# Moving most loads and the early stores of a 3x3 convolution to GpSimd's software DMA queue, each DMA as one packet per engine

## The chip, the core and the metric

The kernel runs on one core of a Trainium2 chip. The metric is the device time of one execution in microseconds. Three runs of the kernel before gave 122.27, 122.31 and 122.54 us; the median is 122.31 us.

The core has a matrix engine (TensorE, PE), a vector engine (VectorE, DVE), a scalar engine (ScalarE, ACT), a general engine (GpSimd, POOL) and an engine that here only issues transfers (SyncE, SP). Data moves between HBM and the on-chip memory (SBUF) through 16 DMA engines that all queues share. TensorE writes to a separate accumulator memory, PSUM.

## The reference

A 3x3 convolution with padding 1 over 16 images of 64 channels and 64x64 pixels, to 64 output channels, plus a residual. All inputs and the output are float32.

```python
def reference(x, weight, residual):
    x_pad = np.pad(x, ((0, 0), (0, 0), (1, 1), (1, 1)), mode='constant')
    for b in range(batch):          # 16
        for co in range(c_out):     # 64
            for ci in range(c_in):  # 64
                for kh in range(3):
                    for kw in range(3):
                        output[b, co] += weight[co, ci, kh, kw] * x_pad[b, ci, kh:kh+h, kw:kw+w]
    return output + residual
```

x, the residual and the output are 16.8 MB each, the weights 0.15 MB: 50.5 MB cross the DMA engines.

## The kernel before

**Tiles.** The 16 images are taken as 8 pairs. A tile of x is one pair: 128 rows (two images of 64 channels), one row of 4096 float32 (16 KB) in each partition, 2 MB in all. Three buffers `xr` hold x (`NXR = 3`), so x of pair p goes into the buffer that pair p - 3 had. The residual has room for all 8 pairs in one tile `ro`; the sum is made in place there, and the stores read it. The residual comes in seven DMAs, listed in `RES` (line 41): pair 0, pair 1, pairs 2 and 3, pairs 4 and 5, pair 6, and the two halves of pair 7. The output leaves in four early stores (`EARLY`, line 39: pairs 0-1, 2-3, 4-5, 6) and, at the end, the two halves of pair 7.

**Work of the engines.** POOL clears an identity matrix, the padding rows of the four bfloat16 tiles `xp`, and two parts of the weight tile `wl` (lines 163 to 179). TensorE turns the weights by nine transposes (line 233), and DVE (line 206) and ACT (line 199) copy the blocks to `wl`, together. For each of 16 images ACT casts x to bfloat16 in two halves, the even rows (line 190) and the odd rows (line 194); TensorE does 24 matmuls for it (lines 100 and 101 by way of a helper) into one of two PSUM tiles; DVE adds the residual in two halves (line 220).

ACT's queue is in this order: issue of residual 0, the two casts of image 0, the weight blocks, the casts of image 1, the casts of image 2, and so on. The casts of image 1 so come behind the weight blocks, and these behind the transposes, which wait for the weights (`s_w`). From image 4 on a cast also waits until TensorE is done with the image that had the same `xp` tile (`s_conv`).

**The order of the DMAs.** SP's queue carries nearly all of them, in the order of the code from line 144: x of pair 0 and, from ACT, residual 0, both put at the very front of the program by `to_the_front`; then the weights; then x of pair 1, residual 1, x of pair 2, x of pair 3, residual 2-3, x of pair 4, x of pair 5, residual 4-5, x of pair 6, x of pair 7, residual 6, residual 7 left, residual 7 right; then the early stores, which first wait for the next-to-last residual load (line 157). From pair 3 on the load of x waits for its buffer:

```python
nc.sync.wait_ge(s_half, 2 * (p - NXR) + 3)      # line 147
```

`s_half` counts ACT's first-half casts (line 190), one for each image. For pair 3 the wait is for 3: the first half of image 2 has been cast, so both images of pair 0 are done and `xr` 0 is free. For pair 4 it is 5, and so on. Each early store waits on `s_add`, which counts the adds of DVE (line 159). The two last stores stand behind the block of hand-ordered work (line 259), after all engines have come to its end; `s_out` counts the early stores, and POOL waits for it at the close (line 261).

Completion of a load is counted on a semaphore: `s_x` (one for each x buffer), `s_r` (three in turn), `s_w`.

Of the kernel before, what the change touches and what calls it, by code (L numbers as in the profile page):

```python
# [15 lines left out]
def kernel(  # L16
# [7 lines left out]
    nc = tc.nc  # L24
# [6 lines left out]
    NPIX = H * W  # L31
    NPAIR = B // 2
# [3 lines left out]
    NXR = 3  # L36
    NXP = 4
    NZERO = 4 + 2 * NXP
    EARLY = (slice(0, 2), slice(2, 4), slice(4, 6), slice(6, 7))
    WHOLE, LEFT, RIGHT = slice(0, NPIX), slice(0, NPIX // 2), slice(NPIX // 2, NPIX)  # L40
    RES = (
        (slice(0, 1), WHOLE, None),
        (slice(1, 2), WHOLE, 1),
        (slice(2, 4), WHOLE, 3),
        (slice(4, 6), WHOLE, 5),
        (slice(6, 7), WHOLE, 7),
        (slice(7, 8), LEFT, 7),
        (slice(7, 8), RIGHT, 7),
    )
    NR = 3  # L50

    res_bc = residual.rearrange("(p b) c h w -> (b c) p (h w)", b=2)
    out_bc = out.rearrange("(p b) c h w -> (b c) p (h w)", b=2)
    x_bc = x.rearrange("b c h w -> (b c) (h w)")
# [6 lines left out]
    ro = pool.tile([128, NPAIR, NPIX], FP32)  # L61
# [6 lines left out]

    sem = lambda name: tc.alloc_semaphore(name)
    s_w = sem("s_w")  # L70
    s_x = [sem(f"s_x{i}") for i in range(NXR)]
    s_r = [sem(f"s_r{i}") for i in range(NR)]
    s_out = sem("s_out")
    s_id = sem("s_id")
    s_half = sem("s_half")
# [2 lines left out]
    s_conv = sem("s_conv")  # L78
    s_add = sem("s_add")

    def load_x(p):
        return nc.sync.dma_start(out=xr[p % NXR][:, :], in_=x_bc[128 * p : 128 * p + 128, :]).then_inc(s_x[p % NXR], 16)

    def load_ro(i, e):
        pairs, cols, _ = RES[i]
        if i >= NR:
            e.wait_ge(s_r[i % NR], 16 * (i // NR))
        return e.dma_start(out=ro[:, pairs, cols], in_=res_bc[:, pairs, cols]).then_inc(s_r[i % NR], 16)

    def wait_ro(e, i):  # L90
        e.wait_ge(s_r[i % NR], 16 * (i // NR + 1))

    def store(pairs, cols=slice(0, NPIX)):
        return nc.sync.dma_start(out=out_bc[:, pairs, cols], in_=ro[:, pairs, cols])

    def matmul(out_, lhsT, rhs, start, stop, ldweights):

# [18 lines left out]
    def to_the_front(dma):  # L116

        def fixed(ap):  # L120
            t = ap.bass_ap.tensor.name
            return mybir.PhysicalAccessPattern(
                ap=ap.ap, offset=ap.bass_ap.offset, dtype=ap.dtype, memref=t, memsetref=t + "_set", bass_ap=ap.bass_ap
            )

        front = nc.main_func.blocks[0].instructions
        here = nc.cur_bb.bb.instructions
        ins = here.pop()
        assert ins.name == dma.ins.name
        at = next(i for i, e in enumerate(front) if e.engine == ins.engine)  # L130
        front.insert(at, copy.replace(ins, ins=[fixed(a) for a in ins.ins], outs=[fixed(a) for a in ins.outs]))
# [9 lines left out]

    with tc.tile_critical(no_gpsimd_drain=True):  # L142

        for p in range(NPAIR):
            if p >= NXR:

                nc.sync.wait_ge(s_half, 2 * (p - NXR) + 3)
            if p == 0:
                to_the_front(load_x(p))
                nc.sync.dma_start(out=wraw[:, :], in_=w_rows[:, :]).then_inc(s_w, 16)  # L150
            else:
                load_x(p)
            for i, (_, _, behind) in enumerate(RES):
                if behind == p:
                    load_ro(i, nc.sync)

        wait_ro(nc.sync, len(RES) - 2)
        for pairs in EARLY:
            nc.sync.wait_ge(s_add, 2 * pairs.stop + 1)
            store(pairs).then_inc(s_out, 16)  # L160


        nc.gpsimd.memset(ident[:, :], 0.0).then_inc(s_id, 1)  # L163
        nc.gpsimd.wait_ge(s_id, 1)
        nc.gpsimd.affine_select(  # L165
            out=ident[:, :],
            in_=ident[:, :],
            compare_op=mybir.AluOpType.not_equal,
            fill=1.0,
            base=0,  # L170
            pattern=[[-1, 128]],
            channel_multiplier=1,
        ).then_inc(s_id, 1)
        nc.gpsimd.wait_ge(s_id, 2)
        for t in xp:
            nc.gpsimd.memset(t[0:64, 0, :], 0.0).then_inc(s_id, 1)  # L176
            nc.gpsimd.memset(t[64:128, J, :], 0.0).then_inc(s_id, 1)  # L177
        nc.gpsimd.memset(wl[0:64, 0, :, 1, :], 0.0).then_inc(s_id, 1)  # L178
        nc.gpsimd.memset(wl[64:128, 1, :, 0, :], 0.0).then_inc(s_id, 1)  # L179


        to_the_front(load_ro(0, nc.scalar))
        for n in range(B):
            p, im = divmod(n, 2)
            hp = slice(64 * im, 64 * im + 64)
            x4 = xr[p % NXR].rearrange("q (j two w) -> q j two w", two=2, w=W)
            t = xp[n % NXP]
            if im == 0:
                nc.scalar.wait_ge(s_x[p % NXR], 16 * (p // NXR + 1))
            i = nc.scalar.copy(out=t[64:128, 0:J, :], in_=x4[hp, :, 0, :])  # L190
            i.then_inc(s_half, 1)
            if n >= NXP:
                i._wait_ge(s_conv, n - NXP + 1)
            nc.scalar.copy(out=t[0:64, 1 : J + 1, :], in_=x4[hp, :, 1, :]).then_inc(s_pack, 1)  # L194
            if n == 0:
                nc.scalar.wait_ge(s_id, NZERO + 1)
                for b in blocks[4:]:
                    for h in range(2):
                        i = nc.scalar.copy(**weight_block(h, *b))  # L199
                i.then_inc(s_id, 1)  # L200


        nc.vector.wait_ge(s_id, NZERO + 1)
        for k, b in enumerate(blocks[:4]):
            for h in range(2):
                i = nc.vector.tensor_copy(**weight_block(h, *b))  # L206
                if k == h == 0:
                    i.then_inc(s_bank, 2)
        i.then_inc(s_id, 1)
        for n in range(B):  # L210
            p, im = divmod(n, 2)
            hp = slice(64 * im, 64 * im + 64)
            o4 = ro[:, p, :].rearrange("q (j two w) -> q j two w", two=2, w=W)
            psj = ps[n % 2].rearrange("q c j w -> q (c j) w")
            if im == 0:
                for i, (pairs, cols, _) in enumerate(RES):
                    if pairs.start <= p < pairs.stop:
                        wait_ro(nc.vector, i)
            for par in range(2):
                i = nc.vector.tensor_tensor(  # L220
                    out=o4[hp, :, par, :], in0=psj[64 * par : 64 * par + 64, :, :], in1=o4[hp, :, par, :], op=ADD
                )
                if par == 0:
                    i._wait_ge(s_conv, n + 1)

                i.then_inc(s_add if par == 0 or n == B - 1 else s_bank, 1)


        nc.tensor.wait_ge(s_id, NZERO)
        nc.tensor.wait_ge(s_w, 16)  # L230
        wraw3 = wraw.rearrange("p (ci t) -> p ci t", t=9)
        for t in range(9):
            i = nc.tensor.transpose(  # L233
                out=tp[0:32, t // 3, 128 * (t % 3) : 128 * (t % 3) + 128], in_=wraw3[:, :, t], identity=ident[:, :]
            )
        i.then_inc(s_id, 1)
        nc.tensor.wait_ge(s_id, NZERO + 3)
        with nc.Fori(0, B // NXP, 1, engines=[PE]):
            for n in range(NXP):
                nc.tensor.wait_ge(s_bank, 1).then_inc(s_bank, -1)  # L240
                nc.tensor.wait_ge(s_pack, 1).then_inc(s_pack, -1)  # L241
                order = [(1, 0), (1, 1), (0, 0), (0, 1), (2, 0), (2, 1)]
                for i, (kw, d) in enumerate(order):
                    xlo, xhi = max(0, 1 - kw), min(W, W + 1 - kw)
                    for c in range(NCHUNK):
                        j0 = JC * c
                        m = matmul(
                            ps[n % 2][:, c, :, xlo:xhi],
                            wl[:, d, kw, :, :].rearrange("q r c -> q (r c)"),
                            xp[n][:, j0 + d : j0 + d + JC, xlo + kw - 1 : xhi + kw - 1],  # L250
                            i == 0,
                            i == len(order) - 1,
                            c == 0,
                        )
                m.then_inc(s_conv, 1)


    for cols in (LEFT, RIGHT):
        store(slice(NPAIR - 1, NPAIR), cols)
    with tc.tile_critical(sync_engine=mybir.EngineType.Pool, no_gpsimd_drain=True):  # L260
        nc.gpsimd.wait_ge(s_out, 16 * len(EARLY))
        tc.free_semaphores([s_w, *s_x, *s_r, s_out, s_id, s_half, s_pack, s_bank, s_conv, s_add])


# [28 lines left out]
```

## Time and profile before

| | before |
|---|---|
| median of three runs | 122.31 us |
| the profiled execution, its time | 122.44 us |
| the profiled execution, its span | 120.6 us |
| DMA | 50.48 MB in 3808 packets, mean 419 GB/s over the span |
| TensorE | 87.7 us busy, first transpose at 12.61 us, first matmul of the convolution at 18.12 us |
| last vector add ends | 108.6 us |
| mean granted TensorE clock | 0.952 |

The issues of the DMA view, with the time from issue to landing (median where there are several):

```profile
xr<-in_x_dram SPq DMA_DIRECT2D x8, 2048.0 KB, 14.4
out_dram<-ro SPq DMA_DIRECT2D x3, 4096.0 KB, 19.2
ro<-in_residual_dram SPq DMA_DIRECT2D x2, 4096.0 KB, 20.7
ro<-in_residual_dram ACTq DMA_DIRECT2D x1, 2048.0 KB, 12.0
wraw<-in_weight_dram SPq DMA_DIRECT2D x1, 144.0 KB, 11.4
```

"SPq" and "ACTq" are the queues of SP and ACT. A landing time counts from the issue until the DMA's semaphore is complete; it holds the time in which the DMA stands behind others. "q1" and "q10" on the page are the DMA queues that SP and ACT use. Engine names with a q at the end mean an engine's instruction queue. "GB/s" is what all DMA engines moved in one of 40 slices of the span; "DMA" is the tenths in which they were busy.

### The profile page before, as it was taken

Reading aid. Unit: us, or ns where it says so; the run is one execution under the profiler, and the core shown is the slowest. Engines: PE = TensorE matmul, PEld = TensorE weight load, DVE = VectorE, ACT = ScalarE, POOL = GpSimd, SP = SyncE. Lnnn points to the kernel's source line nnn. Section 1 sums busy time; section 2 is a strip of 40 time slices with the busy share of each in tenths; the row PEclk is TensorE's granted clock in tenths of the full one; section 3 lists DMA queues with packets and bytes.
Section 4 is the critical chain, followed back from the end, with each engine's and each line's share of the span. In section 5 each row is a group of like instructions: output and inputs, shape, how many; then the busy total and the mean of one; then the engine's idle time right before and its main releaser. Section 6 shows DMA issues by size and latency. Waiting matters only on the chain.

```text
span 120.6 us, 734 instructions
## 1 busy us (share of the span) xinstructions
PE 87.7 (73%) x389; PEld 10.7 (9%) x105; DVE 76.0 (63%) x40; ACT 63.1 (52%) x37; POOL 2.4 (2%) x16
## 2 busy tenths in 40 slices
PE   0000609999999999999999999999999999400000
PEld 0000300111101110101010101010101010000000
DVE  0000080039898898988989898898988989890000
ACT  4001999999988595875959578595800000000000
POOL 5200000000000000000000000000000000000000
PEclk9999999999999999999999999999999999995555
DMA  7999999999999999999999999999999999999994
GB/s 239 429 424 429 430 429 429 429 435 435 435 429 429 424 429 424 429 435 424 435 429 435 435 435 418 421 459 435 429 429 429 429 429 435 435 435 429 399 427 168
DMA packets 3808, 50.48 MB, mean 419 GB/s; under 512 B 352, under 2 KB 480, under 8 KB 480
## 3 DMA queue, kind: packets, MB, share of 16 engines
q1 hardware_dynamic: 3664, 48.38, 94.2%
q10 hardware_dynamic: 144, 2.10, 4.1%
HBM read 33.70 MB, written 16.78 MB: 419 GB/s over the span
## 4 chain that ended last, share of the span: by engine, by line
PE 71%; DVEq 2%; DVE 2%; issue 0%
PE ps L101 54%; PE ps L100 17%; DVEq L142 2%; DVE ro L220 2%
## 5 line engine op out<-in xcount | busy, mean ns | idle before, releaser
L220 DVE TENSOR_TENSOR ro<-ps,ro 64x2048 f32<-64x2048 f32 x32 | 73.2, 2288 | 17.7 <-PE ps L101 17.2
L101 PE MATMUL ps<-xp,wl 128*128 128x504 bf16 (+1 forms) x288 | 80.0, 388 | 0.2
L190 ACT CAST xp<-xr 64x2048 bf16<-64x2048 f32 x16 | 30.3, 1896 | 22.5 <-PE ps L101 13.1
L100 PE MATMUL ps<-xp,wl 128*128 128x504 bf16 (+1 forms) x92 | 35.9, 390 | 3.4 <-PEq L241 3.4
L194 ACT CAST xp<-xr 64x2048 bf16<-64x2048 f32 x16 | 30.4, 1898 | 0.4
L100 PEld LDWEIGHTS ps<-xp,wl 128*128 128x128 bf16 x96 | 9.5, 99 | 79.1 <-issue 79.1
L206 DVE CAST wl<-ps 32x192 bf16<-32x192 f32 x8 | 2.8, 348 | 14.9 <-PE ps L233 14.8
L233 PE MATMUL ps<-ident,wraw 128*32 128x128 f32 x9 | 2.1, 412 | 12.6 <-DMA wraw<-in_weight_dram 12.6
L233 PEld LDWEIGHTS ps<-ident,wraw 128*32 128x32 f32 x9 | 1.2, 137 | 13.0 <-issue 12.6
L190 ACT ACT_TABLE_LOAD x1 | 1.3, 1283 | 1.1 <-SPq L142 1.1
L199 ACT CAST wl<-ps 32x192 bf16<-32x192 f32 x4 | 1.2, 306 | 0.0
L177 POOL MEMSET xp<- 64x64 bf16 x4 | 0.6, 146 | 0.2
L176 POOL MEMSET xp<- 64x64 bf16 x4 | 0.6, 144 | 0.2
L165 POOL TENSOR_SCALAR_AFFINE_SELECT ident<-ident 128x128 f32<-128x128 f32 x1 | 0.3, 292 | 0.2 <-POOL ident L163 0.2
L179 POOL MEMSET wl<- 64x192 bf16 x1 | 0.3, 253 | 0.1
L178 POOL MEMSET wl<- 64x192 bf16 x1 | 0.3, 251 | 0.1
L163 POOL MEMSET ident<- 128x128 f32 x1 | 0.2, 204 | 0.7 <-SPq L142 0.7
L277 POOL MEMSET const-bfloat16-1.0<- 128x1 bf16 x1 | 0.1, 111 | 0.0
L277 POOL MEMSET const-uint8-127<- 128x1 uint8 x1 | 0.1, 111 | 0.0
L277 POOL MEMSET const-float32-1.0<- 128x1 f32 x1 | 0.1, 108 | 0.0
L277 POOL MEMSET const-float32-0.0<- 128x1 f32 x1 | 0.1, 103 | 0.2 <-issue 0.2
## 6 DMA issues: line engine op xcount, KB each, us to landing
xr<-in_x_dram SPq DMA_DIRECT2D x8, 2048.0 KB, 14.4
out_dram<-ro SPq DMA_DIRECT2D x3, 4096.0 KB, 19.2
ro<-in_residual_dram SPq DMA_DIRECT2D x2, 4096.0 KB, 20.7
ro<-in_residual_dram SPq DMA_DIRECT2D x2, 2048.0 KB, 18.1
ro<-in_residual_dram ACTq DMA_DIRECT2D x1, 2048.0 KB, 12.0
ro<-in_residual_dram SPq DMA_DIRECT2D x2, 1024.0 KB, 18.8
out_dram<-ro SPq DMA_DIRECT2D x1, 2048.0 KB, 13.7
out_dram<-ro SPq DMA_DIRECT2D x2, 1024.0 KB, 9.4
```

The source lines that it names most:

```text
L100: return e.matmul(out=out_, lhsT=lhsT, rhs=rhs, start=start, stop=stop, skip_group_check=True)
L101: return e.add_instruction(mybir.InstMatmult(name=nc.get_next_instruction_name(), engine=PE, ins=[e.lower_ap(rhs), e.lower_ap(lhsT)], outs ...
L142: with tc.tile_critical(no_gpsimd_drain=True):
L176: nc.gpsimd.memset(t[0:64, 0, :], 0.0).then_inc(s_id, 1)
L177: nc.gpsimd.memset(t[64:128, J, :], 0.0).then_inc(s_id, 1)
L190: i = nc.scalar.copy(out=t[64:128, 0:J, :], in_=x4[hp, :, 0, :])
L194: nc.scalar.copy(out=t[0:64, 1 : J + 1, :], in_=x4[hp, :, 1, :]).then_inc(s_pack, 1)
L199: i = nc.scalar.copy(**weight_block(h, *b))
L206: i = nc.vector.tensor_copy(**weight_block(h, *b))
L220: i = nc.vector.tensor_tensor(out=o4[hp, :, par, :], in0=psj[64 * par : 64 * par + 64, :, :], in1=o4[hp, :, par, :], op=ADD)
L233: i = nc.tensor.transpose(out=tp[0:32, t // 3, 128 * (t % 3) : 128 * (t % 3) + 128], in_=wraw3[:, :, t], identity=ident[:, :])
L277: nc = _bacc.Bacc("TRN2", target_bir_lowering=False, num_devices=1)
```

## The change

All DMAs behind the first two (x of pair 0 and residual 0) and the weights, up to and with the early stores, are issued by GpSimd and not by SP. GpSimd issues them behind its memsets, in the same order and with the same waits as SP did. A DMA that GpSimd issues [...]is marked `single_packet`: the share of each DMA engine in it is one packet. The two first loads get semaphores of their own (`s_x0`, `s_r0`), so that no semaphore counts DMAs of both kinds. SP keeps x of pair 0, the weights, and the two stores of pair 7.

```diff
+    s_x0, s_r0 = sem("s_x0"), sem("s_r0")
+    s_x = [sem(f"s_x{i}_sw") for i in range(NXR)]
+    s_r = [sem(f"s_r{i}_sw") for i in range(NR)]
...
+    def dma(e, out, in_):
+        return e.dma_start(out=out, in_=in_, single_packet=e is nc.gpsimd)
+
+    def at_x(p):
+
+        return (s_x[p % NXR], 16 * ((p - 1) // NXR)) if p else (s_x0, 0)
+
+    def at_ro(i):
+        return (s_r[i % NR], 16 * ((i - 1) // NR)) if i else (s_r0, 0)
+
+    def load_x(p, e):
+        return dma(e, xr[p % NXR][:, :], x_bc[128 * p : 128 * p + 128, :]).then_inc(at_x(p)[0], 16)
 
     def load_ro(i, e):
         pairs, cols, _ = RES[i]
+        s, before = at_ro(i)
+        if before:
+            e.wait_ge(s, before)
+        return dma(e, ro[:, pairs, cols], res_bc[:, pairs, cols]).then_inc(s, 16)
...
+    def store(pairs, cols, e):
+        return dma(e, out_bc[:, pairs, cols], ro[:, pairs, cols])
...
-        for p in range(NPAIR):
-            if p >= NXR:
-
-                nc.sync.wait_ge(s_half, 2 * (p - NXR) + 3)
-            if p == 0:
-                to_the_front(load_x(p))
-                nc.sync.dma_start(out=wraw[:, :], in_=w_rows[:, :]).then_inc(s_w, 16)
-            else:
-                load_x(p)
-            for i, (_, _, behind) in enumerate(RES):
-                if behind == p:
-                    load_ro(i, nc.sync)
-
-        wait_ro(nc.sync, len(RES) - 2)
-        for pairs in EARLY:
-            nc.sync.wait_ge(s_add, 2 * pairs.stop + 1)
-            store(pairs).then_inc(s_out, 16)
+        to_the_front(load_x(0, nc.sync))
+        nc.sync.dma_start(out=wraw[:, :], in_=w_rows[:, :]).then_inc(s_w, 16)
...
         nc.gpsimd.memset(wl[64:128, 1, :, 0, :], 0.0).then_inc(s_id, 1)
+        for p in range(1, NPAIR):
+            if p >= NXR:
+
+                nc.gpsimd.wait_ge(s_half, 2 * (p - NXR) + 3)
+            load_x(p, nc.gpsimd)
+            for i, (_, _, behind) in enumerate(RES):
+                if behind == p:
+                    load_ro(i, nc.gpsimd)
+
+        wait_ro(nc.gpsimd, len(RES) - 2)
+        for pairs in EARLY:
+            nc.gpsimd.wait_ge(s_add, 2 * pairs.stop + 1)
+            store(pairs, WHOLE, nc.gpsimd).then_inc(s_out, 16)
...
             if im == 0:
-                nc.scalar.wait_ge(s_x[p % NXR], 16 * (p // NXR + 1))
+                s, before = at_x(p)
+                nc.scalar.wait_ge(s, before + 16)
...
     for cols in (LEFT, RIGHT):
-        store(slice(NPAIR - 1, NPAIR), cols)
+        store(slice(NPAIR - 1, NPAIR), cols, nc.sync)
```

More of the change, by code (lines that the diff above doesn't have):

```diff
@@ L70 @@
     s_w = sem("s_w")
-    s_x = [sem(f"s_x{i}") for i in range(NXR)]
-    s_r = [sem(f"s_r{i}") for i in range(NR)]
+    s_x0, s_r0 = sem("s_x0"), sem("s_r0")
+    s_x = [sem(f"s_x{i}_sw") for i in range(NXR)]
+    s_r = [sem(f"s_r{i}_sw") for i in range(NR)]
     s_out = sem("s_out")
@@ L79 @@
     s_add = sem("s_add")
-    def load_x(p):
-        return nc.sync.dma_start(out=xr[p % NXR][:, :], in_=x_bc[128 * p : 128 * p + 128, :]).then_inc(s_x[p % NXR], 16)
+    def dma(e, out, in_):
[6 more added lines that the diff above has]
+        return dma(e, xr[p % NXR][:, :], x_bc[128 * p : 128 * p + 128, :]).then_inc(at_x(p)[0], 16)
     def load_ro(i, e):
         pairs, cols, _ = RES[i]
-        if i >= NR:
-            e.wait_ge(s_r[i % NR], 16 * (i // NR))
-        return e.dma_start(out=ro[:, pairs, cols], in_=res_bc[:, pairs, cols]).then_inc(s_r[i % NR], 16)
+        s, before = at_ro(i)
+        if before:
+            e.wait_ge(s, before)
+        return dma(e, ro[:, pairs, cols], res_bc[:, pairs, cols]).then_inc(s, 16)
     def wait_ro(e, i):
-        e.wait_ge(s_r[i % NR], 16 * (i // NR + 1))
-    def store(pairs, cols=slice(0, NPIX)):
-        return nc.sync.dma_start(out=out_bc[:, pairs, cols], in_=ro[:, pairs, cols])
+        s, before = at_ro(i)
+        e.wait_ge(s, before + 16)
+    def store(pairs, cols, e):
+        return dma(e, out_bc[:, pairs, cols], ro[:, pairs, cols])
     def matmul(out_, lhsT, rhs, start, stop, ldweights):
@@ L258 @@
     for cols in (LEFT, RIGHT):
-        store(slice(NPAIR - 1, NPAIR), cols)
+        store(slice(NPAIR - 1, NPAIR), cols, nc.sync)
     with tc.tile_critical(sync_engine=mybir.EngineType.Pool, no_gpsimd_drain=True):
         nc.gpsimd.wait_ge(s_out, 16 * len(EARLY))
-        tc.free_semaphores([s_w, *s_x, *s_r, s_out, s_id, s_half, s_pack, s_bank, s_conv, s_add])
+        tc.free_semaphores([s_w, s_x0, s_r0, *s_x, *s_r, s_out, s_id, s_half, s_pack, s_bank, s_conv, s_add])
 _INS = ['x', 'weight', 'residual']
```

## The prediction, made before the changed kernel ran

> **What bounds the kernel now.** I read the page's parts 1 to 3 first, then the DMA view by window, then the timeline of the first 24 us, because the chain of waits alone misleads here.
>
> The page, parts 1 to 4:
>
> ```profile
> span 120.6 us, 734 instructions
> PE 87.7 (73%) x389; PEld 10.7 (9%) x105; DVE 76.0 (63%) x40; ACT 63.1 (52%) x37; POOL 2.4 (2%) x16
> ...
> DMA  7999999999999999999999999999999999999994
> ...
> q1 hardware_dynamic: 3664, 48.38, 94.2%
> q10 hardware_dynamic: 144, 2.10, 4.1%
> ...
> PE 71%; DVEq 2%; DVE 2%; issue 0%
> ```
>
> No compute engine is busy over 73%, while the 16 DMA engines are in the top digit in all slices but the first and the last. The chain ends in TensorE work only because it stops at the last vector add (108.7 us); the 12 us behind that are stores. 50.48 MB at the 431 GB/s that the windows view gives for 20 to 100 us are 117.1 us; first byte and last receipt make up the 120.6. So the span is the time to move the bytes, and it grows by every microsecond in which the DMA engines have nothing queued. The question is whether the change makes such a gap.
>
> The DMA view of 3 to 10 us, while two queues compete:
>
> ```profile
> DMA packets 180, 2.95 MB, mean 421 GB/s; under 512 B 0, under 2 KB 0, under 8 KB 0
> ## 3 DMA queue, kind: packets, MB, share of 16 engines
> q1 hardware_dynamic: 96, 1.57, 52.4%
> q10 hardware_dynamic: 84, 1.38, 46.0%
> ```
>
> q1 is SP, with x of pair 0; q10 is ACT, with residual 0. They get packet for packet (1.57 MB / 96 = 16.4 KB, one row of a tile), although SP issued first: the engines take turns.
>
> The timeline of 11 to 24 us (start, duration):
>
> ```profile
> 11.54 1.90 ACT L190 CAST xp<-xr 64x2048 bf16<-64x2048 f32 x1 [9.19 <-DMA xr<-in_x_dram]
> ...
> 12.61 2.08 PE L233 MATMUL ps<-ident,wraw 128*32 128x128 f32 x9 [12.61 <-DMA wraw<-in_weight_dram]
> 13.46 1.90 ACT L194 CAST xp<-xr 64x2048 bf16<-64x2048 f32 x1
> 14.80 2.89 DVE L206 CAST wl<-ps 32x192 bf16<-32x192 f32 x8 [14.80 <-PE ps L233]
> 15.27 1.26 ACT L199 CAST wl<-ps 32x192 bf16<-32x192 f32 x4
> 16.55 1.89 ACT L190 CAST xp<-xr 64x2048 bf16<-64x2048 f32 x1
> 18.12 0.59 PE L100 MATMUL ps<-xp,wl 128*128 128x512 bf16 x1 [3.44 <-PEq L241]
> 18.46 1.90 ACT L194 CAST xp<-xr 64x2048 bf16<-64x2048 f32 x1
> 20.39 1.90 ACT L190 CAST xp<-xr 64x2048 bf16<-64x2048 f32 x1
> 22.31 0.33 SPq L82 DMA_DIRECT2D xr<-in_x_dram  x1
> ```
>
> This is the loop that keeps the DMA fed. Weights land at 12.5; transposes; block copies on DVE and ACT; ACT casts image 1 and the first half of image 2; that third count of s_half releases x of pair 3 (22.31). By the DMA view's issues x of pair 2 lands at 2.58 + 24.5 = 27.1: when pair 3 is issued, some 4.4 us of work is still queued (27.1 less 0.4 for the receipt: in the trace's packet records the weights' last packet is at 12.1, their landing at 12.5). That is the whole margin.
>
> **What the Trainium skill says.** "DMA: Bandwidth & Descriptors", section "Queues, rings and completion order": each DMA engine goes round the queues that have work and drains a whole packet of one before it switches. The trace agrees for packets of one row (96 against 84 above); no packet of many rows is in it. The same page, "Latency and other measured facts": first byte about 0.6 us on the hardware path, about 1 us on GpSimd's. In the trace the first hardware bytes come 1.0 us after issue; the software path is not in it. The same page, "Why small descriptors are slow": about 3 cycles per packet. "SBUF — State Buffer", "SBUF: two separate sides": VectorE in a 2-port mode, or with two SBUF inputs against a GpSimd read, can hold GpSimd off its descriptors. Line 220 reads one operand from PSUM and takes 2288 ns for 2048 elements, so I see no such mode, and cost that at nothing.
>
> **The change, part by part.** Sums are against the profiled execution: span 120.6 us, its time 122.44, so 1.84 us lie around the span; the median of the runs is 122.31, 0.13 lower.
>
> 1. Of SP's 21 DMAs 17 go to POOL (seven of x, six of the residual, four early stores), in the same order with the same waits. SP keeps x of pair 0, the weights and the two last stores; ACT keeps residual 0. Bytes are unchanged.
>
> 2. POOL first does its memsets, which end at 4.04 us. SP issued x1, r1 and x2 at 1.5 to 3.0 us. With about 1 us to first byte the new queue has work at 5 to 6 us. x0, r0 and the weights are 4.34 MB, 10 us of DMA work from 1.0 us on, so this later start alone leaves no gap. Cost nothing; if GpSimd took over 7 us more for its first DMA, the cover is gone.
>
> 3. What competes with the weights. Before, x1, r1 and x2 stood behind x0 and the weights on the same queue. Now they are on a third queue. One row takes 16384 B / (431/16 GB/s) = 0.61 us on an engine; a whole x tile is 8 rows per engine, 4.9 us, and now one packet. At 5.5 us about four of eight rows of x0 are through. From there each engine gives POOL 4.9 us, then one row to SP and one to ACT, then POOL again. SP needs at least a dozen more turns (the rest of x0, its semaphore write, eight 1152 B weight rows, theirs), and POOL has three packets before it stops at s_half. So POOL drains x1, r1 and x2 first, and the weights are last of the six transfers. The six take as long as before, so the last lands near 27.1: weights at 27.1 instead of 12.5 (1.11 + 11.4), plus 14.6. The last row of x0 comes behind the third packet: 6 + 3 × 4.9 + six rows of 0.61 = 24.4, 25 with the receipt, instead of 11.5.
>
> 4. The loop behind it, by the durations above: transposes 27.2 to 29.3; ACT has by then cast image 0 (25 + 3.8 = 28.8) and goes on at 29.4: block copies 1.26, then three casts of 1.90 and their gaps, 5.75: third count of s_half at 36.4 (22.3 before). GpSimd's first byte 1.0 later: 37.4. The queues had run dry at 27.1 − 0.4 = 26.7. Gap: 10.7 us, with nothing beside it.
>
> 5. What is late next. TensorE starts 14.3 us late (29.4 + 2.9 = 32.3), ends at 118.3, the adds at 123.0. The DMA is late by 10.7. Every later wait keeps its cover: x4 needs s_half near 44.1 (29.99 + 14.1) and the queue is full to 52.0 (37.4 + 4.9 + 9.7 for pairs 2 and 3 of the residual); early store 4:6, issued at 90.74, moves to 105.0, and the store ahead of it lands at 78.8 + 21.4 + 10.7 = 110.9. The last two stores are issued at about 123.0 and 123.6; one alone needs some 3.4 us, so 127; the bytes end later, at 119 + 10.7 = 129.7 (in the windows view nothing moves behind 119.0). The DMA stays the bound.
>
> 6. One packet instead of many rows. The nearest bounds: nothing, or 3 cycles at the page's 0.85 GHz, 3.5 ns, per row. POOL moves 44 of 50.48 MB, 168 rows per engine: 0.6 us. I take −0.5, an estimate. The other way, the page's "Measured" section has 425 GB/s for 16 MB on GpSimd's path; 44 MB take 103.5 us so, 102.1 at 431: 1.4 us slower. Neither is in the trace.
>
> 7. SP loses its waits; nothing else stood behind them. POOL's waits stand before nothing but its own DMAs and the closing wait on s_out.
>
> Sum: 120.6 + 10.7 − 0.5 = 130.8 span, + 1.84 = 132.6 us.
>
> **Rivals.**
>
> Row by row (20%): the one-packet mark doesn't make engines hold the turn, and three queues share by rows. Then x0's rest costs 9 turns (to 11.9), its semaphore write and r0's last row 4 (14.3), and each of eight weight rows waits for one POOL row, 5.3 us: 19.6, landing 20.0, 7.5 late. s_half reaches three near 29.2, first byte 30.2, gap 3.5: 122.44 + 3.5 = 125.9 us. For it: the trace shows turns of one row. Against: its DMAs have one row per packet, and the change asks for another packet.
>
> Not slower (10%): the turn is not even; an engine serves SP's and ACT's queues first and POOL's only when they are empty. It decides from the point where POOL gets no turn on an engine before the last weight row, at about 12 us. Then x0 and the weights land as before, POOL's three packets fill the time behind them as SP's did, the loop closes at 22.3, and only item 6 is left: 122.44 − 0.5 = 121.9 us. For it: the page on order speaks of even turns, but no view shows a software queue beside a hardware one. Against: the two hardware queues got even turns although one was first.
>
> Slower still (8%): the gap as forecast, and the software queue also moves less (item 6's 1.4 us instead of a gain) or writes descriptors too late to stay ahead: 134.5 to 138.
>
> **How the numbers follow.** 62% for the forecast: 132.6, its own range 130 to 134.5 (one us to first byte could be 0.5 to 2; item 6 both ways). Range: down to 124.5, to hold the row-by-row case, and up to 135: it leaves out the 10% that is not slower and part of the 8%. What a measurement here can tell from no change is 0.2%, 0.25 us. Faster 0.08, within 0.03, slower 0.89.
>
> **What would show it.** PE's first transpose near 27 us instead of 12.6; a hole of about 10 us in the DMA and GB/s rows from 27 to 37; POOL's x of pair 3 issued at about 36; full DMA digits behind that; packets per queue far fewer, or much larger. A transpose near 20 us means rows in turn; one at 12.6 means I am wrong about who competes. If the DMA row has no hole but GB/s stand under 425, the software path's rate is the cause.

## The result, and the profile after

The changed kernel takes 127.75 us (median of four runs, 127.58 to 127.77), beside 122.38 us for the kernel before (here of four runs): 1.0435 times as long, 95% interval 1.0417 to 1.0453. It is slower by 5.4 us. The profiled execution took 127.76 us, with a span of 125.4.

From the page of the changed kernel, parts 1 to 3 (the rows of slices have 3.1 us for each digit):

```profile
span 125.4 us, 734 instructions
PE 87.6 (70%) x389; PEld 10.7 (9%) x105; DVE 76.0 (61%) x40; ACT 63.2 (50%) x37; POOL 12.4 (10%) x33
...
DMA  7999999934999999999999999999999999999994
GB/s 230 428 423 428 431 437 423 428 162 115 392 423 434 444 428 439 423 423 428 439 439 434 428 418 434 418 405 410 481 428 423 418 423 418 470 434 423 395 442 178
...
q0 software_dynamic: 3088, 44.04, 82.7%
q1 hardware_dynamic: 576, 4.34, 8.6%
q10 hardware_dynamic: 144, 2.10, 3.9%
```

q0, which the page calls software_dynamic, is GpSimd's queue; q1 is SP's and q10 ACT's, as before. TensorE, VectorE and ScalarE are as busy as before, in microseconds; GpSimd has 10 us more, the issuing of its DMAs; the bytes are the same. The DMA row, which had a 9 in every slice but the ends, now has a 3 and a 4: a hole between 25 and 31 us. The windows view of the changed kernel puts a size on it (after the window come the busy times of PE, PEld, DVE, ACT and POOL; the last three columns are the granted clock, the DMA share and GB/s):

```profile
26.80:30.80 4.00, 4.00 (x12) 0.40 (x3) 0.00 (x0) 3.95 (x3) 1.23 (x2) 1.00 0.25 49
30.80:124.00 93.20, 79.58 (x366) 8.88 (x91) 73.24 (x32) 48.99 (x26) 7.15 (x12) 0.95 1.00 425
124.00:125.40 1.40, 0.00 (x0) 0.00 (x0) 0.00 (x0) 0.00 (x0) 0.00 (x0) 0.50 0.00 0
```

Four microseconds move 49 GB/s, about a ninth of what comes behind them; afterwards the DMA engines are full again until 124.0 (119.0 before), and the tail is as long as before. The hole's cause stands in the timeline of the first 30 us (start, duration):

```profile
4.02 0.68 POOL L83 DMA_DIRECT2D xr<-in_x_dram  x1
4.70 0.54 POOL L83 DMA_DIRECT2D ro<-in_residual_dram  x1
5.23 0.53 POOL L83 DMA_DIRECT2D xr<-in_x_dram  x1
13.41 1.90 ACT L202 CAST xp<-xr 64x2048 bf16<-64x2048 f32 x1 [11.05 <-DMA xr<-in_x_dram]
...
19.38 2.08 PE L245 MATMUL ps<-ident,wraw 128*32 128x128 f32 x9 [19.38 <-DMA wraw<-in_weight_dram]
21.50 1.27 ACT L211 CAST wl<-ps 32x192 bf16<-32x192 f32 x4 [4.27 <-PE ps L245]
...
22.79 1.90 ACT L202 CAST xp<-xr 64x2048 bf16<-64x2048 f32 x1
...
24.90 0.59 PE L113 MATMUL ps<-xp,wl 128*128 128x512 bf16 x1 [3.44 <-PEq L253]
...
26.63 1.90 ACT L202 CAST xp<-xr 64x2048 bf16<-64x2048 f32 x1
...
28.82 0.53 POOL L83 DMA_DIRECT2D xr<-in_x_dram  x1 [23.06 <-ACT xp L202]
```

The weights, which landed at 12.5 before, let TensorE go at 19.38. ACT sat idle for 4.27 us before its weight blocks, and the casts behind them came late by nearly as much as the weights: the transposes are 6.8 us late, and x of pair 3 was issued 6.5 us late, at 28.82 instead of 22.31. By then the first six transfers had been over for 2 us.

Why the weights are late is seen in the DMA view of 8.3 to 13 us of the changed kernel (queue: packets, MB, share):

```profile
DMA packets 141, 2.06 MB, mean 439 GB/s; under 512 B 15, under 2 KB 15, under 8 KB 15
...
q0 software_dynamic: 47, 0.77, 38.2%
q10 hardware_dynamic: 47, 0.77, 38.2%
q1 hardware_dynamic: 47, 0.52, 26.2%
```

Three queues get the same number of packets. A packet of GpSimd's queue is 0.77 MB / 47 = 16.4 KB, one row, although its DMAs are marked as one packet. SP's turns here still carry x of pair 0; its small ones are semaphore writes. In the packet records the weights' rows then stand one by one, each behind a 16 KB row of GpSimd's queue.

### The profile page after: what moved, and what is told of

Read it like the earlier page. It is cut to its first block, busy times and chain, and to the rows that moved or that the text cites. A ratio compares the mean times of both kernels' runs of the same rounds, so it can differ in the third digit from the quotient of the medians.

```text
span 125.4 us, 734 instructions
## 1 busy us (share of the span) xinstructions
PE 87.6 (70%) x389; PEld 10.7 (9%) x105; DVE 76.0 (61%) x40; ACT 63.2 (50%) x37; POOL 12.4 (10%) x33
## 2 busy tenths in 40 slices
DMA packets 3808, 50.48 MB, mean 402 GB/s; under 512 B 352, under 2 KB 480, under 8 KB 480
## 3 DMA queue, kind: packets, MB, share of 16 engines
q0 software_dynamic: 3088, 44.04, 82.7%
## 4 chain that ended last, share of the span: by engine, by line
PE 68%; DVEq 2%; DVE 2%; issue 0%
PE ps L114 52%; PE ps L113 16%; DVEq L155 2%; DVE ro L232 2%
## 5 line engine op out<-in xcount | busy, mean ns | idle before, releaser
L83 POOL DMA_DIRECT2D xr<-in_x_dram x7 | 3.9, 560 | 56.8 <-ACT xp L202 56.8
L83 POOL DMA_DIRECT2D out_dram<-ro x4 | 2.7, 679 | 37.6 <-DVE ro L232 22.5
L83 POOL DMA_DIRECT2D ro<-in_residual_dram x6 | 3.5, 590 | 0.0
```

The lines of the kernel that those rows point to most:

```text
L83: return e.dma_start(out=out, in_=in_, single_packet=e is nc.gpsimd)
```

## The experiments

### Does the mark matter?

```diff
-        return e.dma_start(out=out, in_=in_, single_packet=e is nc.gpsimd)
+        return e.dma_start(out=out, in_=in_, single_packet=False)
```

> The changed kernel with the one-packet mark taken off GpSimd's DMAs. If the mark does nothing to the turns of the DMA engines and nothing to the rate (the changed kernel's records show rows of 16 KB in turn on three queues): the weights land near 19.3 us, the hole in the DMA is the same, 127.7 us (within 0.3). If the mark does hold the turn for several rows, or saves time per row, without it the weights land earlier or the full stretches get slower: a change of 0.5 us or more either way.

Measured: 127.79 us (127.63 to 127.99), beside 127.75 for the changed kernel: no difference. The hole is the same: 157 and 94 GB/s in the two low slices of its page. The same question on the hardware path, first with the weights alone marked:

```diff
-        nc.sync.dma_start(out=wraw[:, :], in_=w_rows[:, :]).then_inc(s_w, 16)
+        nc.sync.dma_start(out=wraw[:, :], in_=w_rows[:, :], single_packet=True).then_inc(s_w, 16)
```

> The changed kernel with the one-packet mark also on the weights' DMA, which SP issues. If a marked DMA is one turn on the hardware path: its eight rows of an engine go in one turn and not in eight, the weights land about 4.2 us earlier (near 15.1), the third count of s_half near 24.4, no hole, 122.9 to 123.5. If the mark changes no turns on the hardware path either: weights at 19.3, 127.7.

Measured: 127.58 us (127.35 to 127.98); the timeline of this run has

```profile
19.20 2.08 PE L245 MATMUL ps<-ident,wraw 128*32 128x128 f32 x9 [19.20 <-DMA wraw<-in_weight_dram]
```

so the weights came when they came unmarked. And with all x, residual and output DMAs of the kernel before marked, on their hardware queues:

```diff
-        return nc.sync.dma_start(out=out_bc[:, pairs, cols], in_=ro[:, pairs, cols])
+        return nc.sync.dma_start(out=out_bc[:, pairs, cols], in_=ro[:, pairs, cols], single_packet=True)
...
```

> The kernel before with the one-packet mark on all loads of x and of the residual and on the stores, all still on the hardware queues of SP and ACT (the weights unmarked). If the mark saves the gap between rows (one row each 607 ns in the records[...]): up to 0.9 us less, 121.4. If a marked DMA is one turn, x of pair 0 (or residual 0) comes in one piece, so x lands at about 7 us or stays near 11.5. If the mark does nothing: 122.34, landings as before.

Measured: 122.33 us (13 runs) beside 122.43 for before (17 runs), ratio 0.9992, interval 0.9983 to 1.0000. Its DMA view of 3 to 10 us:

```profile
q1 hardware_dynamic: 96, 1.57, 52.4%
q10 hardware_dynamic: 89, 1.46, 48.7%
```

Rows still alternate, as in the kernel before. With rows of 16 KB (and of 1152 B for the weights) the mark changed neither turns nor rate on either path. Whether the request gets lost, or the engines don't heed it, no run here tells.

### Is it the software queue, or who stands beside the weights?

The three loads that competed with the weights go back to SP, behind the weights; GpSimd issues all from x of pair 3 on. They have semaphores of their own.

```diff
         nc.sync.dma_start(out=wraw[:, :], in_=w_rows[:, :]).then_inc(s_w, 16)
+        load_x(1, nc.sync)
+        load_ro(1, nc.sync)
+        load_x(2, nc.sync)
...
-        for p in range(1, NPAIR):
+        for p in range(NXR, NPAIR):
```

> The changed kernel with x of pairs 1 and 2 and residual 1 back on SP, behind the weights; GpSimd issues everything from x of pair 3 on, marked. Theory A (the loss is the hole in the DMA between 26.8 and 30.7 us, because the weights share turns with GpSimd's first three loads): weights land at 12.5, x of pair 3 is issued at 22.4, no hole or one under 1 us, and the time is that of before plus at most 0.6 us that lies outside the span: 122.4 to 123.0. Theory C (GpSimd's queue moves less, or pauses at each wait): 124 or more, with holes or lower GB/s behind 30 us.

Measured: 122.41 us (122.26 to 122.53, 13 runs), ratio to before 1.0004, interval 0.9996 to 1.0012. GpSimd's queue then carries the later loads and the early stores at the old pace: no digit of the DMA row is under 9 between the ends.

```profile
DMA  6999999999999999999999999999999999999994
GB/s 217 429 435 422 437 429 435 435 424 424 435 429 435 435 435 429 424 429 429 435 429 435 435 429 405 432 451 429 435 435 429 429 424 424 418 435 424 435 421 187
```

So the software queue costs nothing that shows in the steady part. The other way round, all of GpSimd's DMAs stay and the weights move to ACT's queue, ahead of residual 0, which so loses its place at the very front of the program:

```diff
-        nc.sync.dma_start(out=wraw[:, :], in_=w_rows[:, :]).then_inc(s_w, 16)
...
-        to_the_front(load_ro(0, nc.scalar))
+        nc.scalar.dma_start(out=wraw[:, :], in_=w_rows[:, :]).then_inc(s_w, 16)
+        load_ro(0, nc.scalar)
```

> The changed kernel with the weights issued by ACT ahead of residual 0 (both behind the start of the program, at 1.1 and 1.5 us); GpSimd's DMAs stay as they are and still compete with x of pair 0. Theory A: weights land near 3 us, x of pair 0 near 11, third count of s_half near 22, no hole, 122.4 to 123.0. Theory C (the software queue itself costs, wherever the weights stand): 125 or more.

Measured: 123.49 us (123.40 to 123.70). x of pair 3 was issued at 20.26, and no hole is left in the DMA row of the page:

```profile
20.26 0.53 POOL L83 DMA_DIRECT2D xr<-in_x_dram  x1 [14.65 <-ACT xp L202]
```

```profile
DMA  7999999999999999999999999999999999999994
```

x of pair 0 was cast from 7.97 us on, so it landed earlier than I had said, and the transposes began at 8.25, so the weights landed later than I had said. In the packet records the weights' rows lie between 5.03 and 7.79 us and GpSimd's first row begins at 7.85: the two did not meet. Of the 1.1 us that remain over the kernel before, about 0.5 are in the span (121.0; the first slice of its page moves 179 GB/s instead of 239, and ACT issues residual 0 at 1.36 us, not at 0.12), which I had not allowed for, and 0.6 lie around the span, for which I had; they are treated below. Of the loss of 5.4 us, 4.3 are gone.

Last, late weights without any software queue: the kernel before, with the weights behind x of pair 1, and behind x of pair 2.

```diff
             if p == 0:
                 to_the_front(load_x(p))
-                nc.sync.dma_start(out=wraw[:, :], in_=w_rows[:, :]).then_inc(s_w, 16)
             else:
                 load_x(p)
+            if p == 1:                  # the second run: 2
+                nc.sync.dma_start(out=wraw[:, :], in_=w_rows[:, :]).then_inc(s_w, 16)
```

> The kernel before, no software queue at all, with the weights put behind x of pair 1 on SP. If late weights are enough, whoever delays them: weights land near 17.9 us instead of 12.5, the third count of s_half comes near 27.1, first bytes 1.0 later, while the queue is dry at 26.7: a hole of 1.4 us and a restart of 0.5 to 1.0, 124.2 to 124.9. If the loss needs the software queue: 122.4.

> The kernel before, no software queue, with the weights put behind x of pair 2 on SP, so that they are last of the six early transfers, as the prediction had it. By the prediction's own sum the hole is 10.7 us: 133.1; with the restart that the changed kernel showed (1.0): up to 134.2. If the sum of steps is wrong, and not only its premise, the time is under 131 or over 136.

Measured: 124.59 us (124.51 to 124.67) and 134.35 us (134.09 to 134.62). Of the second, the DMA row and three lines of the timeline:

```profile
DMA  6999999800079999999999999999999999999994
```

```profile
2.54 0.49 SPq L153 DMA_DIRECT2D wraw<-in_weight_dram  x1
27.22 2.08 PE L234 MATMUL ps<-ident,wraw 128*32 128x128 f32 x9 [27.22 <-DMA wraw<-in_weight_dram]
36.38 0.33 SPq L82 DMA_DIRECT2D xr<-in_x_dram  x1
```

In the first of the two the transposes began at 17.55 us and x of pair 3 was issued at about 26.7; the packet records have no bytes from 26.78 to 27.69. Late weights alone make such a hole and such a loss, whoever delays them, and the prediction's sum holds where its premise does: weights last give transposes at 27.22 (forecast 27.2), x of pair 3 at 36.38 (36.4), and in the packet records no bytes from 26.76 to 37.35 us (26.7 to 37.4).

### Is the first hole the whole loss?

ACT's weight blocks move behind its casts of image 2, so that x of pair 3 is released without waiting for the weights:

```diff
-            if n == 0:
+            if n == 2:
                 nc.scalar.wait_ge(s_id, NZERO + 1)
```

> The changed kernel with ACT's weight blocks moved behind its casts of image 2; nothing of the DMAs is moved. Theory A (the late weights cost only because ACT's casts, and so the release of x of pair 3, stand behind the weight blocks): weights still land at 19.3, third count of s_half near 23.0, first bytes of x of pair 3 near 24.5, no hole, 122.4 to 123.0 although TensorE starts 1 to 2 us later still (26 to 27). Theory B (TensorE's late start costs): 128.5 to 130.

Measured: 127.14 us (126.84 to 128.18). Both theories missed. The first hole is gone, but others came. Three windows of this run:

```profile
24.00:32.00 8.00, 5.67 (x19) 0.60 (x5) 0.32 (x1) 5.66 (x7) 0.33 (x1) 1.00 1.01 430
46.00:50.00 4.00, 4.00 (x20) 0.39 (x5) 3.39 (x3) 2.63 (x2) 1.15 (x2) 1.00 0.72 217
66.00:70.00 4.00, 4.00 (x20) 0.39 (x4) 3.39 (x3) 2.61 (x3) 2.09 (x4) 1.00 0.84 283
```

GpSimd's own lines show what waited:

```profile
45.92 0.53 POOL L83 DMA_DIRECT2D xr<-in_x_dram  x1 [9.82 <-ACT xp L202]
...
66.67 0.53 POOL L83 DMA_DIRECT2D xr<-in_x_dram  x1 [9.82 <-ACT xp L202]
```

The two lines are x of pairs 5 and 7. x of pair 5 was issued at 45.92, where the kernel before had it at 38.5, because from image 4 on ACT's casts wait for TensorE (`s_conv`), and TensorE began 8.2 us late (26.33). The queue was dry near 46.3. To see this second chain alone, x of pair 3 gets a place that is free anyway, that of residual 7, and waits for nothing:

```diff
+    def x_tile(p):
+        return ro[:, NPAIR - 1, :] if p == NXR else xr[p % NXR][:, :]
...
-            if p >= NXR:
+            if p > NXR:
                 nc.gpsimd.wait_ge(s_half, 2 * (p - NXR) + 3)
```

> The changed kernel with x of pair 3 loaded into the place of residual 7, which is free until late, so that this load waits for nothing. If the hole at 26.8 us were the whole loss: 122.9 (before, plus 0.6 outside the span). Revised theory, from the run with the blocks moved: TensorE stays 6.8 us late, x of pair 5 is then issued at about 45.4 and its first bytes come 1.25 us later, while the queue runs dry near 46.2: a small hole of 0.4 us and a restart of up to 1 us there, 123.3 to 124.5. If TensorE's lateness costs in full: 127 or more.

Measured: 125.82 us (125.52 to 126.44), 1.3 us over the upper end of what the revised theory gave: it saw the loss at 46 us and missed the one at 66.

```profile
24.00:32.00 8.00, 7.25 (x24) 0.79 (x7) 0.32 (x1) 7.90 (x5) 0.00 (x0) 1.00 1.02 436
46.00:50.00 4.00, 4.00 (x21) 0.41 (x5) 3.42 (x2) 2.61 (x3) 0.04 (x1) 1.00 0.99 332
66.00:70.00 4.00, 4.00 (x20) 0.49 (x5) 3.42 (x2) 2.64 (x2) 1.65 (x4) 1.00 0.93 307
```

The DMA engines are hardly idle in these two windows (shares 0.99 and 0.93), yet they move only 332 and 307 GB/s: the queue had run out or was about to, and in the packet records its next rows took up to 1.79 us on an engine, where a row takes 0.61 otherwise. The wait for pair 3 is therefore the gate that sets the loss in the changed kernel, but not the only one that late weights close. With it open, TensorE's late start still costs some 2.9 us, most of it at pairs 5 and 7 (last bytes 122.15 us by the packet records, 119.2 before). In the changed kernel these two waits cost nothing (its packet records show no idle time from 44 to 52 and from 64 to 72 us): by my reading, because the first hole had put the work of the queue ahead of them back as well.

### The time around the span

Between a run's time and its span lie 1.8 us before and 2.36 to 2.57 in the changed kernel. With the three loads on SP GpSimd issues 14 DMAs. On top of that kernel, splitting all early stores by pairs makes it 17 (the edit below), and splitting only the first two makes it 16:

```diff
-    EARLY = (slice(0, 2), slice(2, 4), slice(4, 6), slice(6, 7))
+    EARLY = tuple(slice(p, p + 1) for p in range(NPAIR - 1))
```

> The kernel with the first three loads on SP (122.41), its four early stores split by pairs into seven, so that GpSimd issues 17 DMAs, as many as in the changed kernel, with as many rows as that kernel had with 14. It asks where the 0.6 us outside the span come from (2.45 us lie around the span in the changed kernel, 1.80 here). If from the number of software DMAs: 123.0 with 2.4 us around the span. If from the first three loads (early, or their rows): 122.4, 1.8.

> As the kernel with seventeen software DMAs, with sixteen. If something comes due with the seventeenth: 1.8 us around the span and 122.4. If it grows with the number, or begins at fifteen: 2.0 to 2.5 and 122.6 to 123.2.

| software DMAs | run | median time, us | around the span, us |
|---|---|---|---|
| 0 | before | 122.3 to 122.4 | 1.78 to 1.87 |
| 14 | three loads on SP | 122.41 | 1.75 to 1.84 |
| 16 | split | 123.15 | 2.40 to 2.53 |
| 17 | split | 123.25 | 2.09 to 2.59 |
| 17 | changed kernel | 127.75 | 2.36 to 2.57 |

The spans of the two split kernels are those of before (120.5 to 120.8), so this 0.6 us has nothing to do with the hole. If the number of software DMAs is what counts, it comes with the fifteenth or the sixteenth, not with the seventeenth. But the split also makes DMAs smaller and adds waits, so the cause stays open.

## Why the prediction was right or wrong

Slower was right, and so was the chain from late weights to an empty queue; how the weights come to be late, and so by how much, was wrong. The likeliest value, 132.6, is 4.9 us too high, and the forecast's own range, 130 to 134.5, is missed. 127.75 us lies inside the stated range because that was drawn down to 124.5 for the row-by-row rival, and this rival, held at 20% beside 62% for the forecast, is the case that came.

**What bounds it.** Right: the span follows the time in which the DMA queues are empty (and, which the prediction left out, what the restart adds), and the loop from the weights over ACT to `s_half` makes the hole.

**Step 2, the software queue's start.** Off, and harmless: its first rows are in the records at 8.2 us, 4.2 after the issue at 4.02, not at 5 to 6. The about 1 us that the step took was seen only where the engines were empty (1.25 us, at 28.82); see the end.

**Step 3 failed.** "A whole x tile is 8 rows per engine, 4.9 us, and now one packet": it isn't, and the description of the change above says it wrongly too. Each row took a turn of its own, as in the rival called row by row. GpSimd's queue has 3088 packets, marked or not, and the whole kernel 3808, as before. The prediction's own sign for rows in turn, a transpose near 20 us, came (19.38). The weights landed at 19.2 (1.12 + 18.1) and not at 27.1; x of pair 0 was cast from 13.41 and not from 25. The page "DMA: Bandwidth & Descriptors" of the Trainium skill, section "Queues, rings and completion order", from which I took that an engine drains a whole packet before it switches, is not refuted: no packet of many rows ever appeared. The wrong step was to take the mark for the fact. The diff says what is asked; only the packet counts and sizes in the DMA view say what is done.

**The rival's own sum.** It gave 125.9 us: weights at 20.0 (measured 19.2), first bytes of pair 3 at 30.2 (30.07), hole 3.5 (3.9, idle time averaged over the engines in the packet records). The missing 1.9 us are that 0.4, a restart of about 1.0, and about 0.5 around the span. The restart shows in the landing of pair 3: 22.31 + 9.7 = 32.0 before, 28.82 + 8.0 = 36.8 after, 4.8 later, where the hole alone is 3.9.

**Step 4.** Right given its premise, as the run with the weights last shows: hole 10.6 us for 10.7. Its time, 134.35, is over the 133.1 of the sum by the restart and little more.

**Step 5, later waits.** Right for the changed kernel, where the hole came first. The two runs with the first gate open show that it is right only because of that hole.

**Step 6.** The −0.5 us were nothing: unmarked 127.79, marked 127.75, with the same packets, so nothing was there to be saved. The 1.4 us the other way were nothing too: with the three loads on SP GpSimd's queue kept the pace of the hardware queue (431 GB/s from 32 to 112 us, beside 430 in the kernel before).

## What to carry to other kernels

Moving transfers to another queue takes away an order that the old queue kept: a small load that stood ahead of bulk loads now takes turns with them, and one of many rows waits a turn for each. Before such a move, find the small transfer on whose landing the next issue depends, and keep the bulk behind it in the same queue. When a hole is removed, look again for the next wait that the same late start has moved; its cover may have been the hole.

## What the runs showed of the hardware that I had not expected

- A queue that was empty and got work when other queues already had rows for the DMA engines waited long for its first row, on the software and on the hardware path alike: GpSimd's 4.2 us after its first issue (4.02, 8.18) and, with three loads on SP, 3.6 us (22.64, 26.28); ACT's 4.1 us in the kernel with the weights ahead (0.95, 5.03); SP's 3.3 us for the last stores of the changed kernel (115.53, 118.80). With the queues empty it took 1.25 us on GpSimd's (28.82, 30.07) and 1.0 us on SP's with the weights last (36.38, 37.35). So it is not the cost of a first software DMA; what takes the time while other queues have rows is open.
- A queue that has run dry loses 0.8 to 1.0 us more than the idle time: in the changed kernel the first rows behind the hole took up to 1.64 us on an engine, where a row in the full stretch takes 0.61. With the weights behind x of pair 1 and of pair 2 the same happened on SP's hardware queue (rows of up to 1.89 and 1.83 us).
- Some 0.6 us outside the span were there in the kernels with 16 and 17 software DMAs, and not in those with 14 and none.
